# A decoder trunk on one core: the first loads, the order of the first splits, the adder of the first squares, and one pair of unused transposes in each feed-forward block

## The chip, the core and the metric

The kernel runs on one core of a Trainium2 chip. A core has TensorE (PE, matmuls and, in parallel, the loads of their stationary operand, PEld), VectorE (DVE), ScalarE (ACT), GpSimd (POOL), and SyncE (SP), whose queue issues the DMAs here. The metric is device time in microseconds of one execution, median of several runs.

## The reference, cut to what matters

Two layers over 256 tokens of width 1024. Each layer is a half-step SwiGLU block, a mixing block of 16 attention heads of three kinds, and a second half-step SwiGLU block. The change touches the SwiGLU blocks and the first norm.

```python
def _rmsnorm(x, g):
    y = x32 * lax.rsqrt(jnp.mean(x32 * x32, axis=-1, keepdims=True) + RMS_EPS)
    return (y * g.astype(jnp.float32)).astype(x.dtype)

def _swiglu(x, w_gate, w_up, w_down):
    return (jax.nn.silu(x @ w_gate) * (x @ w_up)) @ w_down

for l in range(DEPTH):                                  # DEPTH = 2, D_FF = 2816
    x = x + 0.5 * _swiglu(_rmsnorm(x, ffn1_norm[l]), ffn1_w_gate[l], ffn1_w_up[l], ffn1_w_down[l])
    h = _rmsnorm(x, mix_norm[l])
    ...
    x = x + concatenate([out_a, out_b, out_c]) @ w_out[l]
    x = x + 0.5 * _swiglu(_rmsnorm(x, ffn2_norm[l]), ffn2_w_gate[l], ffn2_w_up[l], ffn2_w_down[l])
return _rmsnorm(x, final_norm)
```

## The kernel before

x is kept transposed in `xs`, 128 partitions by 8 pieces `k` of 256 tokens. All weights are streamed from HBM by SP in chunks of 128x1024 f32 (512 KB), two chunks to a DMA, into five buffers `raw`. Each chunk is split into a high part `whi` (ACT, L160, rounded to fp32r) and the rest `wlo` (DVE, L161); in the mixing block POOL does some of the latter. A piece of x is split in the same way into the operand pair `xx` (ACT L237 multiplies by the norm's scale and rounds, DVE L238 takes the rest). The factor 1/rms is applied after the products.

A product then is a pair of matmuls (`mm2`): `whi` against both halves of `xx` (512 columns), `wlo` against the high half (256 columns). Below, "a pair" is always these two. All TensorE instructions stand in one fixed order, that in which the program writes them.

The four feed-forward blocks are counted 0 to 3 here (two per layer; the mixing blocks stand between 0 and 1 and between 2 and 3, and block 2 follows block 1 directly). In each, `products(i, h)` makes 8 pairs from one chunk, for `i` from 0 to 21 and the halves `h` 0 and 1: 352 pairs `pgu`. The blocks 0 to 2 then make 176 pairs `pdn`, the last one writes 528 matmuls `pfin` of another form. In the middle of `i` = 2 two breaks stand in TensorE's order: after the first pair the sum of squares is taken into a column (`pss`, four matmuls of one column), and nine pairs later two transposes `prow` (L221, `ident` against a 128x2 column broadcast to 128) make the row of 1/rms. In block 0 there is a third one: before `i` = 6 `make_bias` has two matmuls `pu`.

At the start SP issues the norm's scales (`gain`), then x and the first chunk in rows of 1 KB, of 3 KB and of 4 KB by turns (`FIRST`), then the second chunk and the second pair of chunks one by one. Twelve f32 matmuls of `ident` by itself (`warm`) run on TensorE meanwhile. The first pieces are split in the order of the loop at the end of `tile_trunk`. The squares of x for block 0 (`first_squares`) are made by ACT (L246), added up by POOL (`ss`, L251) and folded (`fold`, L255).

What sets the order: `behind` adds an order without a semaphore between two instructions of an engine; apart from that the program's framework places each engine's instructions by its own estimate. PSUM buffers of the tag `at` rotate over four banks, and a new tenant waits for the readers of the one before.

Of the kernel before, what the change touches and what calls it, by code (L numbers as in the profile page):

```python
# [10 lines left out]
F32 = mybir.dt.float32  # L11
F32R = mybir.dt.float32r
AF = mybir.ActivationFunctionType
OP = mybir.AluOpType

P = 128
D = 1024
T = 256
DEPTH = 2
DK = D // P  # L20
# [16 lines left out]
CH = DK * P  # L37
RAW, SPLIT_AHEAD = 5, 3
WARM = 12
AT = (0, 9)  # L40

FIRST = ((0, 1), (1, 4))

LASTK = 3

# [33 lines left out]


@with_exitstack
def tile_trunk(ctx, tc, xT, gains, kvg, sinks, table, onehot, wgu, wdn, winv, wins, wkv, wout, gfin, out):
    nc = tc.nc

    const = ctx.enter_context(tc.tile_pool(name="const", bufs=1))
    wpool = ctx.enter_context(tc.tile_pool(name="wpool", bufs=2))
    act = ctx.enter_context(tc.tile_pool(name="act", bufs=1))
# [10 lines left out]
    def behind(ins, earlier):  # L98

        if earlier is not None:  # L100
            tc.add_manual_dep(ins.ins, earlier.ins.name,
                              mybir.DependencyInfo(mybir.DependencyClass.NoSync, mybir.DependencyReason.DATA),
                              reason="order of issue")
        return ins


    chunks, loads = [], []
# [20 lines left out]
    raws, parts = {}, {}  # L128
# [18 lines left out]
    def split(n, pieces=1, after=None):  # L147

        if n < len(chunks) and n not in parts:
            load(n)  # L150
            w = chunks[n][2]
            parts[n] = halves_of(n)
            step = w // pieces
            for c in range(0, w, step):
                split_part(n, c, c + step, after)

    def split_part(n, a, b, after=None):
        hi, lo = parts[n]
        low = nc.gpsimd if n in shared else nc.vector
        ops = (nc.scalar.copy(hi[:, a:b], raw(n, a, b)),  # L160
               low.tensor_sub(lo[:, a:b], raw(n, a, b), f(hi[:, a:b])))  # L161
        for op, first in list(zip(ops, after or urgent))[:1 if n in shared else 2]:
            behind(op, first)

    def halves_of(n):
        hi = wpool.tile([P, CH], F32R, tag="whi", name=f"whi{n}", bufs=SPLIT_AHEAD + 1)
# [10 lines left out]
        return parts.pop(n)  # L177


    xs = act.tile([P, DK, T], F32, name="xs")  # L180
    x = [xs[:, k, :] for k in range(DK)]
    gain = const.tile([P, (3 * DEPTH + 1) * DK], F32, name="gain")
    nc.sync.dma_start(out=gain, in_=gains)
    room(0)
    for a, b in FIRST:
        nc.sync.dma_start(out=xs[:, a:b, :], in_=xT[:, a:b, :])
        nc.sync.dma_start(out=raws[0][:, 0, 2 * a * P:2 * b * P], in_=loads[0][:, 0, 2 * a * P:2 * b * P])
    nc.sync.dma_start(out=xs[:, DK // 2:, :], in_=xT[:, DK // 2:, :])
    nc.sync.dma_start(out=raws[0][:, 1, :], in_=loads[0][:, 1, :])
    room(1)  # L190
    for j in range(2):
# [6 lines left out]
    ident = const.tile([P, P], F32, name="ident")  # L198
# [2 lines left out]
                            fill=1.0, base=0, channel_multiplier=1)  # L201
    ones = const.tile([P, 1], F32, name="ones")
    nc.vector.memset(ones, 1.0)
    mhalf = const.tile([P, 2], F32, name="mhalf")
    nc.vector.memset(mhalf, -0.5)

    xx = [act.tile([P, 2, T], F32R, name=f"xx{k}") for k in range(DK)]
    xh = [t[:, 0, :] for t in xx]
# [20 lines left out]
    class Norm:  # L229
        def __init__(self, idx):  # L230
            self.idx, self.sums = idx, []

        def g(self, k):
            return gain[:, self.idx * DK + k:self.idx * DK + k + 1]
# [6 lines left out]
        def square(self, k, last=False, after=None):  # L241

            if k % 2 == 0:
                return
            sq = tmp.tile([P, 2, T], F32, tag="sq2", name="sq", bufs=2)
            behind(nc.scalar.activation(sq, xs[:, k - 1:k + 1, :], AF.Square), after)  # L246
            if len(self.sums) == 0 or (last and k == DK - 1):
                self.sums.append(sq)
            else:
                s = tmp.tile([P, 2, T], F32, tag="ss", name="ss", bufs=2)  # L250
                nc.gpsimd.tensor_add(s, self.sums[0], sq)  # L251
                self.sums = [s]
            if k == DK - (3 if last else 1):
                s = tmp.tile([P, T], F32, tag="fold", name="fold", bufs=1)
                nc.gpsimd.tensor_add(s, self.sums[0][:, 0, :], self.sums[0][:, 1, :])  # L255
                self.sums = [s]
            elif k == DK - 1:
                self.sums = [self.sums[0], sq[:, 0, :], sq[:, 1, :]]
# [33 lines left out]
    def mm2(out, whi, wlo, both, first, last):  # L292

        matmul(out, whi, both.rearrange("p a t -> p (a t)"), start=first, stop=False)
        matmul(out[:, :T], wlo, both[:, 0, :], start=False, stop=last)

    def residual(a, b, p, scale, nxt, last=False):
        nc.vector.scalar_tensor_tensor(xs[:, a:b, :], p, scale, xs[:, a:b, :], op0=OP.mult, op1=OP.add)
        if not last:
            for k in range(a, b):  # L300
                nxt.operands(k)
# [5 lines left out]
        nc.vector.tensor_add(a, p[:, :T], b)  # L307
        return a

    def ffn(norm, nxt, last=False, first=None, between=(), at=AT):  # L310
        hs, banks, ws = [], {}, {}

        def products(i, h, start=0, stop=DK):

            if start == 0:
                ws[0] = next_w(ahead=(i, h) not in ((1, 1), (2, 0)))
                if h == 0:
                    for m in range(2):
                        banks[i, m] = bank("pgu", "at" if i % 3 == 2 else "mm")
            whi, wlo = ws[0]  # L320
            for j in range(start, stop):
                k, m = h * DK // 2 + j // 2, j % 2
                c = slice(j * P, (j + 1) * P)
                mm2(banks[i, m], whi[:, c], wlo[:, c], xx[k], k == 0, k == DK - 1)


        products(0, 0)
        products(0, 1)
        if first:
            first()  # L330
        products(1, 0)
        products(1, 1)
        for n in range(2 * DK):
            products(2, n // DK, n % DK, n % DK + 1)
            if n == at[0]:
                col = norm.column()
                for m in range(2):
                    split(cursor[0] + SPLIT_AHEAD - 2 + m)
            if n == at[1]:
                row = rms_row(col)  # L340
        for i in range(FK):
            if i in between:
                between[i]()
            if i > 2:
                products(i, 0)
                products(i, 1)
            g, u = add_halves(banks.pop((i, 0)), "A"), add_halves(banks.pop((i, 1)), "C")
            t = tmp.tile([P, T], F32, tag="A", name="t")
            nc.vector.tensor_mul(t, g, row)  # L349
            s = tmp.tile([P, T], F32, tag="B", name="s")  # L350
            nc.scalar.activation(s, t, AF.Silu)  # L351
            sr = tmp.tile([P, T], F32, tag="B", name="sr")
            nc.gpsimd.tensor_mul(sr, s, row)  # L353
            h = tmp.tile([P, T], F32, tag="h", name="h", bufs=2)
            nc.vector.tensor_mul(h, sr, u)  # L355
            hs.append(act.tile([P, 2, T], F32R, tag=("hh", "hl")[i % 2], name=f"h{i}", bufs=FK // 2))
            nc.scalar.copy(hs[i][:, 0, :], h)  # L357
            nc.vector.tensor_sub(hs[i][:, 1, :], h, f(hs[i][:, 0, :]))
        if last:
            finish(hs)  # L360
            return
        for k in range(DK):
            p = bank("pdn")
            for kk in range(FK):
                j = (k * FK + kk) % DK
                if j == 0:
                    whi, wlo = next_w()
                c = slice(j * P, (j + 1) * P)
                mm2(p, whi[:, c], wlo[:, c], hs[kk], kk == 0, kk == FK - 1)
            nc.vector.scalar_tensor_tensor(x[k], p[:, T:], 0.5, x[k], op0=OP.mult, op1=OP.add)  # L370
            residual(k, k + 1, p[:, None, :T], 0.5, nxt)
            nxt.square(k)
# [405 lines left out]

    norm = Norm(0)
    parts[0], parts[1] = halves_of(0), halves_of(1)  # L780
    for k in range(DK):
        norm.operands(k)
        if k < DK // 2:
            split_part(0, 2 * k * P, 2 * (k + 1) * P)
        elif k % 2:
            split_part(1, (k - 5) * 2 * P, (k - 3) * 2 * P)
    split(2)
    start = norm

    def first_squares():  # L790
# [2 lines left out]

    for l in range(DEPTH):
        nxt = Norm(3 * l + 1)
        ffn(norm, nxt, first=first_squares if l == 0 else None, between={3: load_bias, 6: make_bias} if l == 0 else {})
        norm, nxt = nxt, Norm(3 * l + 2)
        mix(l, norm, nxt)
        norm, nxt = nxt, Norm(3 * l + 3)
        ffn(norm, nxt, last=l == DEPTH - 1)  # L800
        norm = nxt
# [23 lines left out]
def _layout(x, rel_bias_table, ffn1_norm, ffn1_w_gate, ffn1_w_up, ffn1_w_down, mix_norm, w_in, attn_sinks,  # L825
# [7 lines left out]
    g = np.stack([v for l in range(DEPTH) for v in (ffn1_norm[l], mix_norm[l], ffn2_norm[l])] + [final_norm])  # L833
    gu, dn = [], []
    for l in range(DEPTH):
# [11 lines left out]
    winv = np.moveaxis(rv.reshape(DEPTH, P, 4, 2 * VCOLS), 2, 1)  # L847
# [3 lines left out]
    last = wo[:, -LASTK:].reshape(DEPTH, LASTK, P, DK, P).transpose(0, 3, 1, 2, 4).reshape(DEPTH, LASTK, DK, P, P)  # L851
    wo[:, -LASTK:] = last.transpose(0, 1, 3, 2, 4).reshape(DEPTH, LASTK, P, D)
    return {
        "xT": np.moveaxis(x[0].T.reshape(DK, P, T), 0, 1),
        "gains": np.moveaxis(g.reshape(-1, DK, P), 2, 0).reshape(P, -1),
        "kvg": kv_norm_c.T,
        "sinks": attn_sinks[:, HEADS[:NA]].reshape(1, -1),
        "table": rel_bias_table,
# [27 lines left out]
```

## Time and profile before

| | |
|---|---|
| runs, us | 959.44, 965.29, 961.68 (median 961.68) |
| profiled execution, us | 965.39, its span 963.6 |
| TensorE clock granted | 0.998 |
| PE busy in the span | 951.5 us (99%), 5824 matmuls |
| DVE, ACT, POOL busy | 688.2, 553.9, 178.5 us |
| DMA | 174.92 MB, mean 182 GB/s |
| chain that ended last | PE 93%, DVE 2%, ACT 2%, POOL 1%, DMA 1% |

The page counts an engine as busy while it runs an instruction; matmuls overlap, so a busy PE says nothing of how far apart they start. The chain is followed back from the last instruction to what released each step; where it is made of PE alone, PE's own pace sets the time. Timeline rows give start, duration, engine, line, operation, tiles, and in brackets the idle time before with what ended it.

### The profile page before, as it was taken

How to read it: one execution, taken by the hardware profiler on the slowest of the kernel's cores; microseconds unless marked ns; L12 is line 12 of the kernel's file. 1: busy time of each engine (PE TensorE's matmuls, PEld its weight loads, DVE VectorE, ACT ScalarE, POOL GpSimd, SP SyncE). 2: the span in 40 equal slices, each digit the busy share in tenths (PEclk: the TensorE clock that was granted, in tenths of full speed). 3: DMA queues.
4: the chain of work that ended last, by engine and by line, in shares of the span. 5: the costliest groups of instructions: out<-in, count | busy, mean ns of one | idle time of the engine just before them, and what ended most of it. 6: DMA issues, size and time to landing. Idle time of an engine off the chain costs nothing.

```text
span 963.6 us, 15380 instructions
## 1 busy us (share of the span) xinstructions
PE 951.5 (99%) x5824; PEld 839.2 (87%) x5824; DVE 688.2 (71%) x1228; ACT 553.9 (57%) x1024; POOL 178.5 (19%) x154
## 2 busy tenths in 40 slices
PE   8999999999999999999999999999999999999997
PEld 6888888898999888888888888888989988888885
DVE  5787775658847877775668777666696579777544
ACT  6655554446876665654446555544478576556443
POOL 3221110111312221110113112000222042211000
PEclk9999999999999999999999999999999999999999
DMA  9688555563434555545555555555534455555521
GB/s 335 215 296 302 197 195 175 160 213 111 140 128 138 200 192 191 199 175 178 198 186 182 183 208 178 185 188 176 176 109 153 145 187 193 179 198 191 179 85 44
DMA packets 47718, 174.92 MB, mean 182 GB/s; under 512 B 3307, under 2 KB 5883, under 8 KB 47516
## 3 DMA queue, kind: packets, MB, share of 16 engines
q1 hardware_dynamic: 47356, 173.42, 52.1%
q8 instruction: 45, 0.74, 0.3%
q10 hardware_dynamic: 288, 0.52, 0.1%
q14 instruction: 29, 0.24, 0.1%
HBM read 172.86 MB, written 4.22 MB: 184 GB/s over the span
## 4 chain that ended last, share of the span: by engine, by line
PE 93%; DVE 2%; ACT 2%; POOL 1%; DMA 1%; issue 0%; SPq 0%; POOLq 0%; ACTq 0%
PE pgu L218 50%; PE pdn L218 19%; PE pp L218 7%; PE pfin L218 6%; PE pwo L218 5%; PE pv L218 2%; PE po L218 1%; PE pt L221 1%; PE psc L218 1%; DVE acc L563 1%; DMA raw<-wgu 1%; POOL ss L251 1%; DVE m L562 1%; ACT whi L160 1%; ACT e L640 0%
## 5 line engine op out<-in xcount | busy, mean ns | idle before, releaser
L218 PE MATMUL pgu<-xx,whi 128*128 128x512 f32 x1408 | 494.9, 396 | 1.9 <-ACT whi L160 1.9
L161 DVE TENSOR_TENSOR wlo<-raw,whi 128x1024 fp32r<-128x1024 f32 (+3 forms) x314 | 383.2, 1223 | 145.5 <-ACT whi L160 139.0
L160 ACT CAST whi<-raw 128x1024 fp32r<-128x1024 f32 (+2 forms) x322 | 332.7, 1034 | 251.4 <-PE pdn L218 86.2
L218 PE MATMUL pgu<-xx,wlo 128*128 128x256 f32 x1408 | 395.1, 281 | 0.2 <-DVE wlo L161 0.2
L218 PEld LDWEIGHTS pgu<-xx,whi 128*128 128x128 f32 x1408 | 264.1, 188 | 64.5 <-ACT whi L160 2.5
L218 PEld LDWEIGHTS pgu<-xx,wlo 128*128 128x128 f32 x1408 | 266.1, 189 | 0.8 <-DVE wlo L161 0.8
L218 PE MATMUL pdn<-h,whi 128*128 128x512 f32 x528 | 185.5, 396 | 0.0
L353 POOL TENSOR_TENSOR sr<-s,rrow 128x256 f32<-128x256 f32 x88 | 97.9, 1113 | 355.4 <-ACT s L351 355.1
L218 PE MATMUL pdn<-h,wlo 128*128 128x256 f32 x528 | 148.1, 281 | 0.0
L218 PEld LDWEIGHTS pdn<-h,whi 128*128 128x128 f32 x528 | 99.1, 188 | 23.8
L305 ACT COPY b<-pgu 128x256 f32<-128x256 f32 x176 | 65.4, 372 | 80.8 <-PE pgu L218 80.8
L218 PEld LDWEIGHTS pdn<-h,wlo 128*128 128x128 f32 x528 | 99.8, 189 | 0.0
L307 DVE TENSOR_TENSOR a<-pgu,b 128x256 f32<-128x256 f32 x176 | 73.7, 420 | 25.3 <-ACT b L305 24.7
L218 PE MATMUL pp<-xx,whi 128*128 128x256 f32 x480 | 90.8, 289 | 0.0
L218 PEld LDWEIGHTS pp<-xx,whi 128*128 128x128 f32 x480 | 74.2, 191 | 2.7 <-issue 1.7
L218 PE MATMUL pp<-xx,wlo 128*128 128x256 f32 x240 | 67.7, 282 | 0.0
L355 DVE TENSOR_TENSOR h<-sr,a 128x256 f32<-128x256 f32 x88 | 37.4, 425 | 28.9 <-POOL sr L353 28.5
L218 PE MATMUL pfin<-whi,h 128*128 128x512 f32 x176 | 48.8, 391 | 0.0
L218 PE MATMUL pwo<-ohl,whi 128*128 128x256 f32 x256 | 47.7, 287 | 0.0
L357 ACT CAST h<-h 128x256 fp32r<-128x256 f32 x88 | 35.3, 401 | 18.6 <-DVE h L355 18.6
L218 PEld LDWEIGHTS pp<-xx,wlo 128*128 128x128 f32 x240 | 45.8, 191 | 0.0
L351 ACT ACTIVATE s<-t 128x256 f32<-128x256 f32 x88 | 37.4, 425 | 6.0 <-DVE t L349 5.7
(109 smaller groups left out, 796.0 us busy)
## 6 DMA issues: line engine op xcount, KB each, us to landing
raw<-wgu SPq DMA_DIRECT2D x86, 1024.0 KB, 4.9
raw<-wdn SPq DMA_DIRECT2D x44, 1024.0 KB, 4.9
raw<-wins SPq DMA_DIRECT2D x14, 1024.0 KB, 4.9
raw<-wout SPq DMA_DIRECT2D x8, 1024.0 KB, 4.9
raw<-winv SPq DMA_DIRECT2D x4, 776.0 KB, 4.3
w<-u SPq DMA_DIRECT2D x1, 3072.0 KB, 14.5
bias<-w SPq DMA_DIRECT2D x1, 2048.0 KB, 9.3
raw<-wgu SPq DMA_DIRECT2D x3, 512.0 KB, 7.8
```

Source lines behind the costliest of these rows:

```text
L160: ops = (nc.scalar.copy(hi[:, a:b], raw(n, a, b)), low.tensor_sub(lo[:, a:b], raw(n, a, b), f(hi[:, a:b])))
L161: low.tensor_sub(lo[:, a:b], raw(n, a, b), f(hi[:, a:b])))
L218: in_order(nc.tensor.matmul(*a, **kw))
L221: in_order(nc.tensor.transpose(*a))
L251: nc.gpsimd.tensor_add(s, self.sums[0], sq)
L305: nc.scalar.copy(b, p[:, T:])
L307: nc.vector.tensor_add(a, p[:, :T], b)
L351: nc.scalar.activation(s, t, AF.Silu)
L353: nc.gpsimd.tensor_mul(sr, s, row)
L355: nc.vector.tensor_mul(h, sr, u)
L357: nc.scalar.copy(hs[i][:, 0, :], h)
L562: nc.vector.max(out=m8, in_=acc[:, cs])
```

## The change

It does five things.

- `gains` and x become one DRAM tensor with rows of 56 + 2048 f32 to a partition; the tile `xg` holds both. SP's first DMA brings the scales with the first four pieces of x (rows of 4320 bytes), the next the whole first chunk, then the second half of x, the second chunk, and the second pair of chunks as before.
- `mhalf` is set first, and an ACTIVATE on it that nobody reads (`idle`) is issued ahead of all loads.
- The first splits go half by half: four `xx`, then four quarters of chunk 0, then four `xx`, then four quarters of chunk 1, each ordered behind the last; chunk 2 behind those.
- The adds of the squares of the first norm are done by DVE instead of POOL.
- `step()` writes two transposes of `mhalf`, broadcast to 128 columns, against `ident` into an `at` bank that nobody reads. It is called once in each feed-forward block: in block 0 after `i` = 6, `h` = 0, in the others after three pairs of `i` = 3, `h` = 0.

```diff
-FIRST = ((0, 1), (1, 4))
+STEPS, STEPS0 = ((3, 0, 3),), ((6, 1, 0),)
+GAINS = (3 * DEPTH + 1) * DK
...
-    xs = act.tile([P, DK, T], F32, name="xs")
+    xg = act.tile([P, GAINS + DK * T], F32, name="xs")
+    gain, xs = xg[:, :GAINS], xg[:, GAINS:].rearrange("p (k t) -> p k t", t=T)
     x = [xs[:, k, :] for k in range(DK)]
-    gain = const.tile([P, (3 * DEPTH + 1) * DK], F32, name="gain")
-    nc.sync.dma_start(out=gain, in_=gains)
+    mhalf = const.tile([P, 2], F32, name="mhalf")
+    nc.vector.memset(mhalf, -0.5)
+    nc.scalar.activation(const.tile([P, 2], F32, name="idle"), mhalf, AF.Copy, scale=mhalf[:, 0:1])
+    cut = GAINS + DK // 2 * T
     room(0)
-    for a, b in FIRST:
-        nc.sync.dma_start(out=xs[:, a:b, :], in_=xT[:, a:b, :])
-        nc.sync.dma_start(out=raws[0][:, 0, 2 * a * P:2 * b * P], in_=loads[0][:, 0, 2 * a * P:2 * b * P])
-    nc.sync.dma_start(out=xs[:, DK // 2:, :], in_=xT[:, DK // 2:, :])
+    nc.sync.dma_start(out=xg[:, :cut], in_=xT[:, :cut])
+    nc.sync.dma_start(out=raws[0][:, 0, :], in_=loads[0][:, 0, :])
+    nc.sync.dma_start(out=xg[:, cut:], in_=xT[:, cut:])
     nc.sync.dma_start(out=raws[0][:, 1, :], in_=loads[0][:, 1, :])
...
+            self.adder = nc.gpsimd if idx else nc.vector
...
-                nc.gpsimd.tensor_add(s, self.sums[0], sq)
+                self.adder.tensor_add(s, self.sums[0], sq)
...
-                nc.gpsimd.tensor_add(s, self.sums[0][:, 0, :], self.sums[0][:, 1, :])
+                self.adder.tensor_add(s, self.sums[0][:, 0, :], self.sums[0][:, 1, :])
...
+    def step():
+        p = bank("step", "at")
+        for b in range(2):
+            transpose(p[:, b * P:(b + 1) * P], mhalf[:, b:b + 1].to_broadcast([P, P]), ident)
...
             for j in range(start, stop):
+                if (i, h, j) in steps:
+                    step()
...
-    for k in range(DK):
-        norm.operands(k)
-        if k < DK // 2:
-            split_part(0, 2 * k * P, 2 * (k + 1) * P)
-        elif k % 2:
-            split_part(1, (k - 5) * 2 * P, (k - 3) * 2 * P)
-    split(2)
+    ops = (None, None)
+    for n in range(2):
+        for k in range(n * DK // 2, (n + 1) * DK // 2):
+            norm.operands(k)
+            for op, earlier in zip(norm.ops, ops):
+                behind(op, earlier)
+            ops = norm.ops
+        for c in range(0, CH, CH // 4):
+            ops = split_part(n, c, c + CH // 4, ops)
+    split(2, after=ops)
```

ACT at the start of the program, before: `xx` is the operand pair of a piece of x, `whi` a part of a chunk, `raw` its buffer.

```order
L237 ACT_TABLE_LOAD
L237 ACTIVATE xx_103<-xs,gain 128x256
L160 CAST whi_126<-raw_75 128x256
L237 ACTIVATE xx_104<-xs,gain 128x256
L237 ACTIVATE xx_105<-xs,gain 128x256
L160 CAST whi_126<-raw_75 128x256 x2
L237 ACTIVATE xx_106<-xs,gain 128x256
L160 CAST whi_126<-raw_75 128x256
```

And after the change.

```order
L190 ACT_TABLE_LOAD
L190 ACTIVATE idle<-mhalf 128x2
L243 ACTIVATE xx_101<-xs 128x256
L243 ACTIVATE xx_102<-xs 128x256
L243 ACTIVATE xx_103<-xs 128x256
L243 ACTIVATE xx_104<-xs 128x256
L163 CAST whi_124<-raw_77 128x256 x4
```

The table load moves in front of an instruction that reads only `mhalf`, and the four pieces of x come ahead of the four quarters of the first chunk instead of between them.

DVE from the second chunk on to the sum of squares, after the change (`wlo_161` and `wlo_165` are chunks 2 and 3, `wlo_187` is chunk 4, `ss` and `fold` the adds of the squares).

```order
L164 TENSOR_TENSOR wlo_127<-raw_77,whi_126 128x256 x4
L164 TENSOR_TENSOR wlo_161<-raw_82,whi_160 128x1024
L257 TENSOR_TENSOR ss<-sq 128x512
L164 TENSOR_TENSOR wlo_165<-raw_82,whi_164 128x1024
L257 TENSOR_TENSOR ss<-ss,sq 128x512 x2
L261 TENSOR_TENSOR fold<-ss 128x256
L164 TENSOR_TENSOR wlo_187<-raw_85,whi_186 128x1024
```

The four adds stood on POOL, ahead of `rcol`; now they stand between the splits of chunks 2, 3 and 4 on DVE.

PE in block 0, after the change: the end of `i` = 6, `h` = 0 and the beginning of `h` = 1.

```order
L223 MATMUL pgu<-xx_104,whi_474 128x512
L223 MATMUL pgu<-xx_104,wlo_475 128x256
L226 MATMUL step<-ident,mhalf 128x128 x2
L223 MATMUL pgu<-xx_105,whi_515 128x512
L223 MATMUL pgu<-xx_105,wlo_516 128x256
```

Two matmuls stand between two pairs that followed each other before. In the blocks 1 to 3 the same two stand between the third and the fourth pair of `i` = 3; nothing else in PE's order differs.

## Rows read from the trace of the kernel before

**Rows 1.** The page, part 1: busy us (share of the span) xinstructions.

```profile
PE 951.5 (99%) x5824; PEld 839.2 (87%) x5824; DVE 688.2 (71%) x1228; ACT 553.9 (57%) x1024; POOL 178.5 (19%) x154
```

**Rows 2.** The chain in order of time: start us, us, what.

```profile
2.59 5.81 DMA raw<-wgu
...
14.57 1.80 POOL ss L251
...
20.98 1.60 POOL fold L255
22.62 0.61 PE pss L218 x4
...
137.50 62.19 PE pdn L218 x352
...
315.80 109.54 PE pgu L218 x620
...
503.03 107.48 PE pgu L218 x620
```

**Rows 3.** Waits of PE from 0 to 60 us: us in total, times, longest.

```profile
PE pgu L218 <- ACT whi L160: 1.9, 2, 1.3
...
PE pss L218 <- POOL fold L255: 1.0, 1, 1.0
```

**Rows 4.** The timeline from 0 to 40 us.

```profile
0.74 0.39 SPq L183 DMA_DIRECT2D gain<-gains  x1
...
1.35 5.49 PE L218 MATMUL warm<-ident 128*128 128x128 f32 x24 [1.35 <-POOL ident L200]
...
3.76 1.28 ACT L237 ACT_TABLE_LOAD   x1 [3.76 <-DMA xs<-xT]
...
6.50 0.59 PE L218 MATMUL pgu<-xx,whi 128*128 128x512 f32 x1
...
8.42 0.71 ACT L160 CAST whi<-raw 128x256 fp32r<-128x256 f32 x2
...
9.75 1.71 ACT L237 ACTIVATE xx<-xs,gain 128x256 fp32r<-128x256 f32 x4
...
10.32 1.67 DVE L238 SCALAR_TENSOR_TENSOR xx<-xs,gain,xx 128x256 fp32r<-128x256 f32 x4
...
11.99 1.30 DVE L161 TENSOR_TENSOR wlo<-raw,whi 128x512 fp32r<-128x512 f32 x2
...
12.92 1.03 ACT L160 CAST whi<-raw 128x1024 fp32r<-128x1024 f32 x1
...
13.85 0.63 ACT L246 ACTIVATE sq<-xs 128x512 f32<-128x512 f32 x1
...
15.46 1.99 DVE L161 TENSOR_TENSOR wlo<-raw,whi 128x1024 fp32r<-128x1024 f32 x1 [0.25 <-ACT whi L160]
...
18.52 1.23 DVE L161 TENSOR_TENSOR wlo<-raw,whi 128x1024 fp32r<-128x1024 f32 x1 [1.07 <-ACT whi L160]
```

**Rows 5.** Windows: us, busy (x) of PE, PEld, DVE, ACT, POOL; PEclk, DMA share, GB/s.

```profile
3.25:5.25 2.00, 2.00 (x11) 2.00 (x11) 0.00 (x0) 1.47 (x2) 0.00 (x0) 1.00 0.90 130
...
6.50:13.00 6.50, 4.39 (x21) 2.96 (x21) 4.97 (x12) 5.49 (x14) 0.00 (x0) 1.00 1.02 412
```

**Rows 6.** DMA issues from 689.5 to 694 us: xcount, KB, us to landing.

```profile
raw<-wins SPq DMA_DIRECT2D x1, 512.0 KB, 3.4
```

**Rows 7.** PE groups, 26.05 to 26.2 us: xcount, busy us, mean ns, idle.

```profile
L218 PE MATMUL pgu<-xx,whi 128*128 128x512 f32 x1 | 0.4, 403 | 0.0
```

**Rows 8.** The same, 315.13 to 315.3 us.

```profile
L218 PE MATMUL pgu<-xx,whi 128*128 128x512 f32 x1 | 0.4, 398 | 0.0
```

**Rows 9.** PE's timeline, 26.1 to 27.3 us: block 0's transposes `prow`.

```profile
26.23 0.28 PE L218 MATMUL pgu<-xx,wlo 128*128 128x256 f32 x1
26.35 0.38 PE L221 MATMUL prow<-ident,rcol 128*128 128x128 f32 x2
...
26.93 0.39 PE L218 MATMUL pgu<-xx,whi 128*128 128x512 f32 x1
```

More of the change, by code (lines that the diff above doesn't have):

```diff
@@ L81, in tile_trunk @@
 @with_exitstack
-def tile_trunk(ctx, tc, xT, gains, kvg, sinks, table, onehot, wgu, wdn, winv, wins, wkv, wout, gfin, out):
+def tile_trunk(ctx, tc, xT, kvg, sinks, table, onehot, wgu, wdn, winv, wins, wkv, wout, gfin, out):
     nc = tc.nc
@@ L163, in split_part @@
             behind(op, first)
+        return ops
     def halves_of(n):
@@ L203, in tile_trunk @@
     nc.vector.memset(ones, 1.0)
-    mhalf = const.tile([P, 2], F32, name="mhalf")
-    nc.vector.memset(mhalf, -0.5)
     xx = [act.tile([P, 2, T], F32R, name=f"xx{k}") for k in range(DK)]
@@ L308, in add_halves, with ffn @@
         return a
-    def ffn(norm, nxt, last=False, first=None, between=(), at=AT):
+    def ffn(norm, nxt, last=False, first=None, between=(), at=AT, steps=STEPS):
         hs, banks, ws = [], {}, {}
@@ L795, in tile_trunk @@
         nxt = Norm(3 * l + 1)
-        ffn(norm, nxt, first=first_squares if l == 0 else None, between={3: load_bias, 6: make_bias} if l == 0 else {})
+        if l == 0:
+            ffn(norm, nxt, first=first_squares, between={3: load_bias, 6: make_bias}, steps=STEPS0)
+        else:
+            ffn(norm, nxt)
         norm, nxt = nxt, Norm(3 * l + 2)
@@ L853, in _layout @@
     return {
-        "xT": np.moveaxis(x[0].T.reshape(DK, P, T), 0, 1),
-        "gains": np.moveaxis(g.reshape(-1, DK, P), 2, 0).reshape(P, -1),
+        "xT": np.concatenate([np.moveaxis(g.reshape(-1, DK, P), 2, 0).reshape(P, -1),
+                              np.moveaxis(x[0].T.reshape(DK, P, T), 0, 1).reshape(P, -1)], axis=1),
         "kvg": kv_norm_c.T,
```

## The prediction

> **What bounds the kernel now.** I read the page's busy times first: PE is busy for 951.5 of 963.6 us [rows 1], so only two things can move the end: idle time of PE at either end, and the pace of PE itself. The chain says where the first lies: up to 22.62 us it runs through a DMA, ACT, and then POOL's adds of the squares, and behind `pss` it is PE nearly throughout [rows 2]. The waits of PE name it from the other side: two waits for `whi`, 1.9 us, and one of 1.0 us for `fold` [rows 3]. The timeline gives the first product at 6.50 us [rows 4]. From there to `pss` stand 33 pairs (chunks 0 to 3 and one). At the pace below they need 33 x 0.353 = 11.65 us, and they take 22.62 - 6.50 = 16.12: 4.5 us are lost there.
>
> For the pace, the chain's long PE pieces are divided by their pairs (two matmuls each). Block 0's `pdn`: 62.19 us / 176 = 353.4 ns. Block 1 behind `prow`: 109.54 / 310 = 353.4. Block 2 behind `prow`: 107.48 / 310 = 346.7 [rows 2]. The instructions are alike and nobody is waited for, yet there are two paces, 6.7 ns a pair apart, and each holds for hundreds of pairs, across chunks and from `pgu` into `pdn`. In the slow one the wide matmul's length goes round in three pairs, 403, 398, 395 ns; in the fast one it is 391 throughout. A pace changes only where the stream is broken. Before `prow` of block 0 the last wide matmul was one of 403 ns [rows 7], and behind it the pace was fast; the same row stands before block 2's `prow`, fast behind it too. Before block 1's it was one of 398 ns [rows 8], and the slow pace went on. In block 3 the pace was fast before `prow` and stayed so. So I read the result of a two-transpose break from the place in the round of three at which it falls: after 403 it ends the slow pace (2 of 2), after 398 it does not (1 of 1), and in the fast pace it does no harm (1 of 1).
>
> **The change, part by part.**
>
> *First loads.* SP's first DMA is issued at 0.74 us as before [rows 4]. It is now 553 KB in rows of 4320 bytes. The nearest row is a DMA of 512 KB issued to an idle queue: 3.4 us to landing [rows 6]; the 5% more add 0.1. So x's first half is there at 0.74 + 3.5 = 4.2 us. What follows is queued behind it, 524 KB each at 412 GB/s [rows 5], 1.27 us: chunk 0 at 5.5, the second half of x at 6.8, chunk 1 at 8.0, chunk 2 at 9.3. Before, the same queue moved only 130 GB/s from 3.25 to 5.25 us, with the rows of 1 and 3 KB [rows 5]. Bounds: at 412 GB/s from the first microsecond on, everything 0.9 us earlier; with the same 2 us at 130 instead of 412 GB/s again, 2 x (412 - 130) / 412 = 1.4 us later.
>
> *Table load.* 1.28 us, begun at 3.76, when x had landed [rows 4]. It now waits for a memset only, and lies before 4.2 us under the load: nothing of it is left on the path. If it did stay there, the first split would start at 5.5.
>
> *Order of the splits.* ACT takes 1.71 us for four `xx` and about 0.35 for a quarter (0.71 for two); DVE 1.67 and, from 1.30 for two halves, about 0.35 as well, the first some 0.4 [rows 4]. ACT: `xx` 4.25 to 5.96, chunk 0's quarters to 7.4, `xx` to 9.1, chunk 1's quarters from 9.1, the first done at 9.5, all at 10.45; one `sq` 0.63, chunk 2 1.03 [rows 4], done at 12.1. DVE follows by half a microsecond: the first `wlo` quarter at 6.9, chunk 1's first at 10.0, and chunk 2 at 12.1 + 1.23 = 13.4. PE is held by `warm` until about 6.45 in any case (its rows end at 6.84, the last overlapping [rows 4]), starts there, and has its first narrow matmul at 6.9, as before. Then 8 pairs to 9.7; 0.3 us of waiting for chunk 1's `wlo`; 8 pairs; 0.5 us for chunk 2's; 16 pairs and one: `pss` at 19.2 instead of 22.62. **Minus 3.4 us.** With the loads' bounds put through the same steps `pss` comes at 18.2 or at 20.6: minus 4.4 to minus 2.0.
>
> *Adds on DVE.* POOL took 1.80 us for one add of 128x512 and 1.60 for the fold [rows 2]; PE waited for the last [rows 3]. On DVE a two-input operation of that size costs 0.65 (half of 1.30 [rows 4]), so three and a fold are about 2.4 us. Between chunk 2 at 13.4 and `pss` DVE has `ss` to 14.05, chunk 3 to 15.3, two `ss` to 16.6, `fold` to 17.0: 2.2 us before `pss` asks. Behind them in DVE's queue stands chunk 4, done at 18.2, which PE asks for at 19.0: the cover is 0.8 us, and what goes beyond it would be PE's. One thing comes back: a split of 1.23 us took 1.99 while POOL's add ran [rows 4]. I take zero beyond the wait that is already in the 3.4.
>
> *The steps.* Each is two transposes of the form of `prow`. In block 0 the start of the narrow matmul before `prow` and that of the second wide one behind it are 26.93 - 26.23 = 0.70 us apart [rows 9]; without it, one pair and a narrow-to-wide distance of 0.12 would be 0.47. So 0.23 each, **plus 0.9 us** for four. The bank that each writes has been read long before in the blocks 1 to 3; in block 0 its reader is DVE's sum for the first half of `i` = 5, eight pairs of `i` = 6 back, and in the trace it was over by then.
>
> What they give hangs on where they fall. In block 1 the step comes nine pairs behind `prow`; the wide matmul there is one of 403 ns. In block 0 it comes eight pairs behind `pu`, and there too it is 403 (the row of [rows 7] stands the same at 49.36 and 318.47 us). Both then are breaks of the kind that ended the slow pace. Block 0: 248 pairs `pgu` and 176 `pdn` are left, 424 x 6.7 ns = **minus 2.8 us**. Block 1: 301 + 176, and 33 of block 2 up to its own `pss`, 510 x 6.7 = **minus 3.4 us**. Blocks 2 and 3 are fast already, so there the step is only its price. Bounds: no gain at all, or a loss where a step falls in the fast pace (below).
>
> **The sum** against the profiled execution's own time: 965.39 - 3.4 + 0.9 - 2.8 - 3.4 = **956.7 us**. That execution is the longest of those shown; against their median, 961.68, it is 0.5% less. The three runs spread by 5.85 us, about what the slow stretches of the blocks 0 and 1 are worth together; if some ran with one of them fast, the median holds part of this gain already.
>
> **The rivals.**
>
> *The steps are only a price.* A rule stands beside it: the Trainium skill, "TensorE: Matmul & The Clock Gate", section "Back-to-back issue gap", gives the isolated gap of a matmul from its columns alone, which would make a pair 325 ns (an estimate from its table) whatever stood before; no run here shows that pace. What speaks against the rival is that one stream has two paces and that breaks changed them [rows 2, 7, 8]; what speaks for it is that two breaks are few. Then 965.39 - 3.4 + 0.9 = 962.9.
>
> *One of the two blocks stays slow.* The new start shifts where `pss` of block 0 falls in the round, and the round behind `pu` may differ; block 1 comes out of a mixing block with hundreds of short waits. 956.7 + 2.8 = 959.5, or + 3.4 = 960.1.
>
> *The loads stumble as before.* The long rows meet the same slow stretch that rows of 3 KB met: 1.4 us later, 958.1.
>
> *The other side: a step breaks the fast pace.* In block 2 a step that turned it slow would cost 477 pairs x 6.7 = 3.2 us, in block 3 301 x 6.7 = 2.0. With no gain in the blocks 0 and 1: 962.9 + 5.2 = 968.1, slower than before. It decides from 2.5 us on, that is with block 2 alone. For it: `pu`, a longer break, did turn the fast pace of block 0 into the slow one. Against it: `prow` of block 3, the same two transposes, did not.
>
> **How the numbers follow.** The sum 0.58; one block stays slow 0.18; the loads stumble 0.08; only a price 0.06; the other side 0.04; more than the sum (the better loads, and no waits for chunks 1 and 2: below 955) 0.06. The range 953.5 to 961.0 leaves out the price and the other side, and takes in the bounds of the loads on both sides of the sum. About 1%, 9.6 us, is what a measurement of this kernel can tell from no change. Faster by more needs under 952.1 against the median, or under 955.7 if before is measured like its profiled execution: 0.10. Slower by more needs 971.3: 0.02. The rest, 0.88, is within.
>
> **What would show it.** In the profile after: `ACT_TABLE_LOAD` over before 3 us; first `xx` near 4.2; `pss` near 19.2 with no wait for `fold`; block 0's `pdn` in 61.0 us instead of 62.19, and block 1's pgu piece in some 107.7; wide matmuls of 391 ns behind each step. The prediction is wrong if the first `xx` starts after 5.6, if a wait for chunk 4's `wlo` takes the place of that for `fold`, or if `pdn` of block 0 or 1 still takes 62.2.

## The result, and the profile after

| | before | after |
|---|---|---|
| median of 5 runs each, us | 961.7 (959.44 to 965.29) | 968.37 (968.29 to 968.54) |
| ratio to before, 95% interval | | 1.0057 [1.0031, 1.0082] |
| profiled execution, us | 965.39, its span 963.6 | 968.34, its span 966.5 |

So the change costs 0.6%. By the 1% named above that is no change, but it lies 7.4 us over the upper end of the range, 961.0, and on the other side of before. Each ratio, here and below, is to runs of before taken beside the kernel in question; the median of before was 961.7 to 964.1 us in them.

The page of after, part 1, to be laid beside [rows 1]: PE is busy 5.8 us longer, with eight matmuls more.

```profile
PE 957.3 (99%) x5832; PEld 839.7 (87%) x5832; DVE 687.8 (71%) x1234; ACT 553.5 (57%) x1027; POOL 170.7 (18%) x150
```

The start went as it was meant to. Four rows of the timeline of after from 0 to 40 us (start us, us, what):

```profile
0.73 1.28 ACT L190 ACT_TABLE_LOAD   x1 [0.73 <-PEq L895]
...
4.52 1.71 ACT L243 ACTIVATE xx<-xs 128x256 fp32r<-128x256 f32 x4 [2.20 <-DMA xs<-xT]
...
12.91 0.69 DVE L257 TENSOR_TENSOR ss<-sq 128x512 f32<-128x512 f32 x1
...
16.17 0.42 DVE L261 TENSOR_TENSOR fold<-ss 128x256 f32<-128x256 f32 x1
```

The first DMA of after, then the window from 3.25 to 5.25 us (columns as in [rows 5]): 419 GB/s where before had 130.

```profile
xs<-xT SPq DMA_DIRECT2D x1, 540.0 KB, 3.8
```

```profile
3.25:5.25 2.00, 2.00 (x11) 2.00 (x11) 0.19 (x1) 0.73 (x2) 0.00 (x0) 1.00 1.04 419
```

Of PE's waits in the first 60 us, where before had those of [rows 3], one is left, that of the warm-up for `ident`:

```profile
PE warm L223 <- POOL ident L207: 1.4, 1, 1.4
```

The loss is behind the start. The chain of after:

```profile
18.99 0.34 PE pss L223 x4
...
22.78 19.06 PE pgu L223 x108
...
134.05 62.19 PE pdn L223 x352
...
315.12 106.35 PE pgu L223 x602
421.47 62.19 PE pdn L223 x352
...
502.54 106.35 PE pgu L223 x602
608.89 62.19 PE pdn L223 x352
...
789.98 106.35 PE pgu L223 x602
...
934.48 20.78 PE pfin L223 x89
```

And three pieces of before that [rows 2] did not need:

```profile
610.52 61.01 PE pdn L218 x352
...
787.49 107.47 PE pgu L218 x620
...
932.23 20.21 PE pfin L218 x89
```

Every `pdn` of after takes 62.19 us, 353.4 ns a pair, and each of the three long `pgu` pieces 106.35 us for 301 pairs, 353.3 ns. No step ended the slow pace, and the blocks 2 and 3, fast before, are slow now. The step of block 0 even fell into a fast stretch, the eight pairs behind `pu`, and the slow pace began behind it: the wide matmuls from 44 to 45.9 us, ahead of the step, and from 47 to 50.2 us.

```profile
L223 PE MATMUL pgu<-xx,whi 128*128 128x512 f32 x7 | 2.5, 392 | 0.0
```

```profile
L223 PE MATMUL pgu<-xx,whi 128*128 128x512 f32 x11 | 3.9, 397 | 0.0
```

The slow pace is also not the old one: before's wide matmuls went round in three (403, 398, 395 ns), after's go by turns (0.40 and 0.39 us), the spacing of the pairs being 345 and 361 ns. Even `pfin`, which the change doesn't touch, became longer.

The two spans, stretch by stretch (after minus before, us): up to `pss` -3.6; `pss` to `prow` of block 0 -0.3; `prow` to `pu` +0.3; the rest of block 0 +0.2; first mixing block -0.7; block 1 +0.3; block 2 +3.4; second mixing block -0.6; block 3 up to `pfin` +2.4; `pfin` +1.5; the tail +0.1. That is +2.9 net, the 966.5 - 963.6 of the spans.

What had changed that nobody had written? The tiles had moved. In the built programs the tile of the scales left the constants' pool and went in front of x, and `mhalf` and `idle` changed places with it. So the weight tiles `whi` and `wlo` start 192 bytes lower than before and the operand tiles `xx` and `h` 32 bytes higher. All these tiles have sizes that are multiples of 256 bytes, so in one kernel every weight tile has the same remainder modulo 256, and every operand tile too: before 64 and 64, after 128 and 96. Below, "distance" is operand minus weight modulo 256: 0 before, 224 after. These places are read from the programs, not from a trace. Padding changes no engine's order of instructions: in the built programs every padded kernel below has that of its unpadded version.

### The profile page after: what moved, and what is told of

Its sections match the earlier page's. It is cut to its first block, busy times and chain, and to the rows that moved or that the text cites. A ratio compares the mean times of both kernels' runs of the same rounds, so it can differ in the third digit from the quotient of the medians.

```text
span 966.5 us, 15393 instructions
## 1 busy us (share of the span) xinstructions
PE 957.3 (99%) x5832; PEld 839.7 (87%) x5832; DVE 687.8 (71%) x1234; ACT 553.5 (57%) x1027; POOL 170.7 (18%) x150
## 4 chain that ended last, share of the span: by engine, by line
PE 96%; DVE 2%; ACT 1%; issue 0%; POOL 0%; POOLq 0%; ACTq 0%
PE pgu L223 52%; PE pdn L223 19%; PE pp L223 7%; PE pfin L223 6%; PE pwo L223 5%; PE pv L223 2%; PE po L223 1%; PE pt L226 1%; PE psc L223 1%; DVE acc L576 1%; PE warm L223 1%; DVE m L575 1%; ACT e L653 0%; PE pi L223 0%; PE pss L223 0%
## 5 line engine op out<-in xcount | busy, mean ns | idle before, releaser
L164 DVE TENSOR_TENSOR wlo<-raw,whi 128x1024 fp32r<-128x1024 f32 (+2 forms) x316 | 380.7, 1208 | 147.9 <-ACT whi L163 140.8
```

## The experiments

Each kernel computes the whole output. Where an edit says "no steps" it is `STEPS, STEPS0 = (), ()`. Padding is written as a longer tile of which the old part is used.

**First: the places, or the steps and the new order?** *After with the places of before.*

```diff
-    xg = act.tile([P, GAINS + DK * T], F32, name="xs")
+    xg = act.tile([P, GAINS + DK * T + 8], F32, name="xs")[:, :GAINS + DK * T]
-    mhalf = const.tile([P, 2], F32, name="mhalf")
+    mhalf = const.tile([P, 2 + 48], F32, name="mhalf")[:, 0:2]
```

> The changed kernel with padding alone: 192 bytes more in the small constants and 32 behind x, so that the weight tiles and the operand tiles xx and h start again at 64 modulo 128 bytes, as before the change (the change had moved the weights to 0 and xx and h to 96 modulo 128). Theory A (where the operands lie sets which slow round TensorE can fall into, and whether two transposes end it): the slow round is again of three pairs (361, 349, 350 ns) and the steps end it in the blocks 0 and 1, 955.5 to 958.5 us, pdn of block 0 in 61.0 us. Theory B (the new start and the steps themselves put the stream into the round of two, addresses don't matter): 968 to 969 us, the round of two (345, 361) as in the changed kernel.

964.69 us, 1.0025 [1.0014, 1.0036]: neither theory's number. The round of three is back, and block 2 is fast, but block 0, block 1 and, unlike before, block 3 are slow. Its chain:

```profile
22.85 19.07 PE pgu L223 x108
...
134.16 62.19 PE pdn L223 x352
...
607.40 61.01 PE pdn L223 x352
...
787.73 106.35 PE pgu L223 x602
```

So the places decide which round there is. But this run also tests the prediction's rule on breaks, at the old places. The wide matmul just before `prow` of block 0, in the window from 22.2 to 22.33 us, and `prow` itself from the timeline:

```profile
L223 PE MATMUL pgu<-xx,whi 128*128 128x512 f32 x1 | 0.4, 403 | 0.0
```

```profile
22.47 0.38 PE L226 MATMUL prow<-ident,rcol 128*128 128x128 f32 x2
```

It is one of 403 ns, as in [rows 7], and the 54 pairs behind `prow` take 19.07 us, 353.1 ns each: slow. `prow` of block 1 also came behind 403 ns (window from 311.7 to 311.78 us), and the slow pace went on there too.

```profile
L223 PE MATMUL pgu<-xx,whi 128*128 128x512 f32 x1 | 0.4, 403 | 0.0
```

*Before with only the operand tiles moved, by 32 bytes, as in after.*

```diff
-    xs = act.tile([P, DK, T], F32, name="xs")
+    xs = act.tile([P, DK * T + 8], F32, name="xs")[:, :DK * T].rearrange("p (k t) -> p k t", t=T)
```

> The kernel before with 32 unused bytes behind x, so that xx and h start at 96 modulo 128 as after the change; the weights stay at 64, nothing else moves. Theory A: a round of two pairs, the blocks 2 and 3 slow behind their prow (796 pairs x 6.7 ns = 5.3 us on the profile of before), pfin some 1.4 us longer: 967 to 972 us. Theory B: as before, 959 to 966 us, round of three pairs.

958.64 us, 0.9961 [0.9947, 0.9974]: outside what either theory said, faster instead of slower. Its chain:

```profile
22.56 0.61 PE pss L218 x4
...
135.67 61.01 PE pdn L218 x352
...
603.19 61.01 PE pdn L218 x352
...
779.28 107.47 PE pgu L218 x620
...
924.88 20.78 PE pfin L218 x89
```

All four blocks run at 346.7 ns a pair, with no step and with before's late `pss`. Thirty-two bytes behind x do what the steps were thought to do. Groups of PE from 150 to 190 us show the two paces: first this kernel, then after.

```profile
L218 PE MATMUL pdn<-h,whi 128*128 128x512 f32 x117 | 40.6, 390 | 0.0
```

```profile
L223 PE MATMUL pdn<-h,whi 128*128 128x512 f32 x114 | 40.3, 397 | 0.0
```

*After without steps, and the old places without steps* (the same padding as in the first edit).

```diff
-STEPS, STEPS0 = ((3, 0, 3),), ((6, 1, 0),)
+STEPS, STEPS0 = (), ()
```

> The changed kernel without the four steps, addresses as in the changed kernel. If a step breaks the fast pace that stands behind pu (eight pairs at 346.7 ns in the changed kernel's trace): 424 pairs at 346.7 and four steps of 0.23 us less, 968.4 - 2.8 - 0.9 = 964.6 us. If the steps are a price only: 967.4. If they were what ends a slow pace anywhere: over 968.4.

> As e1 without the steps: the new start with the old addresses. Theory A: the pace is that of the kernel before (blocks 0 and 1 in part slow, 2 and 3 fast), less 3.6 us for the start: 957 to 962 us, and 0 to 5 us above e1, which is what the steps are worth. Theory B: about 967.

967.45 us, 1.0053 [1.0036, 1.007], the number of "a price only", and 963.87, 1.0028 [1.0012, 1.0044], between the two theories. Taking the four steps out gives back 968.37 - 967.45 = 0.9 us and 964.69 - 963.87 = 0.8, and no long stretch changes its pace with them: the first keeps `pdn` at 62.18 to 62.19 us throughout, the second is slow in the blocks 0, 1 and 3 and fast in 2, as with steps. A piece of the first, then two of the second (blocks 2 and 3):

```profile
608.23 62.19 PE pdn L223 x352
```

```profile
499.58 107.47 PE pgu L223 x620
...
784.04 109.53 PE pgu L223 x620
```

In the second, `prow` of block 3 too came behind a wide matmul of 403 ns (window from 783.4 to 783.5 us) and left the slow pace as it was.

**Second: which place counts, that of the weights, that of the operands, or their distance?** Edits on after: `+ 48` and `+ 16` of padding (weights at 64, operands at 96) without and with steps; `+ 48` and none behind x (64 and 32, distance 224 as in after) without steps. And before with 16 elements behind the scales and 24 behind x:

```diff
-    xs = act.tile([P, DK, T], F32, name="xs")
+    xs = act.tile([P, DK * T + 24], F32, name="xs")[:, :DK * T].rearrange("p (k t) -> p k t", t=T)
-    gain = const.tile([P, (3 * DEPTH + 1) * DK], F32, name="gain")
+    gain = const.tile([P, (3 * DEPTH + 1) * DK + 16], F32, name="gain")[:, :(3 * DEPTH + 1) * DK]
```

> The changed kernel without the steps, padded so that the weight tiles start at 64 modulo 128 bytes and xx and h at 96, the two that e2 had (the changed kernel has 0 and 96, the kernel before 64 and 64). If the two starts set the pace: 346.7 ns a pair in all blocks, and e2's time less what the new start gives (pss at 19.0 instead of 22.6 us): 958.6 - 3.6 = 955.0 us. If e2's pace came from something else in the kernel before: 961 to 968.

> As e5 with the four steps. If a step is a price only: e5 + 0.9 us. If it breaks the pace even here: up to 5 to 10 us more than e5. If it gives something: under e5.

> As e5 with xx and h at 32 modulo 128, the weights at 64: the distance from weight to operand is 96 as in the changed kernel, both starts differ from it. If the distance alone matters: the round of two pairs, about 967.5 us. If it matters that the operand lies 32 bytes off a multiple of 64 while the weights lie on an odd multiple of 64: as e5, about 955.

> The kernel before, nothing changed but padding (96 bytes behind the norm's scales, 64 behind x), so that its weight and operand tiles start where the changed kernel has them, at 0 and 96 modulo 128. If the starts alone cost the changed kernel its time: the round of two pairs (345, 361 ns) nearly everywhere, pfin some 1.5 us longer, and the changed kernel's time plus its gain at the start less the steps: 968.4 + 3.6 - 0.9 = 971.1 us. If the loss came from the new start or the steps: 959 to 966 as before.

955.07 us (0.9901 [0.9872, 0.993]) without steps, 955.73 (0.9908 [0.9879, 0.9936]) with them: with weights at 64 and operands at 96 all blocks are fast, and the steps are a price of 0.7 us. The chain of the one without steps:

```profile
22.73 18.73 PE pgu L223 x108
...
131.80 61.01 PE pdn L223 x352
...
599.12 61.01 PE pdn L223 x352
...
775.23 107.48 PE pgu L223 x620
...
920.82 20.77 PE pfin L223 x89
```

Operands at 32 instead of 96, distance 224 at other places than after's: 967.56 us, 1.0034 [1.0017, 1.005], after's round of 345 and 361 ns, and after's chain:

```profile
134.16 62.18 PE pdn L223 x352
...
933.84 20.77 PE pfin L223 x89
```

The last of the four was meant to give before the places of after, and missed its number: 966.82 us, 1.0024 [1.0008, 1.004], and neither of the two paces but a third, 61.60 us / 176 = 350.0 ns. The places had been counted modulo 128; modulo 256 this kernel's weights lie at 128 and its operands at 224, a distance of 96, and not 224 as in after. (The expectation's text names the two paddings the wrong way round; the edit has 64 bytes behind the scales and 96 behind x.) Modulo 128 the two kernels are alike, and their paces are not: that miss shows that 128 is too small a period.

```profile
136.66 61.60 PE pdn L218 x352
...
608.33 61.60 PE pdn L218 x352
```

**Third: the distance again at other weights, and three distances not seen yet.** Without steps: after's own weights with 64 bytes behind x (128 and 160, distance 32), and `+ 48` with `+ 24`, `+ 40`, `+ 56` behind x (weights at 64, distances 64, 128, 192).

```diff
-    xg = act.tile([P, GAINS + DK * T], F32, name="xs")
+    xg = act.tile([P, GAINS + DK * T + 16], F32, name="xs")[:, :GAINS + DK * T]
```

> As e5 with weights and operand tiles both moved by 64 bytes against it: weights at 128 modulo 256, xx and h at 160, so both starts are new and the distance from weight tile to operand tile is 32 modulo 256 as in e2, e5 and e6. If the distance alone sets the pace: 346.7 ns a pair in all blocks, 955 us as e5. If the starts themselves count: another pace, 960 to 968.

> As e5 with the distance from weight tile to operand tile 64 modulo 256 instead of 32 (weights at 64, xx and h at 128). If every distance has a pace of its own: a steady pace between 346.7 and 353.4 ns in all blocks, 955 to 968 us. If only the place inside 64 bytes counts: as distance 0, both paces, round of three, 959 to 964.

> As e10 with distance 128 modulo 256. If the distance counts modulo 128: both paces as at distance 0, 959 to 964 us. If modulo 256 or more: a pace of its own, 955 to 968.

> As e10 with distance 192 modulo 256. If distances just below a multiple of 256 are bad as 224 is: 353.3 ns, about 967 us. If 224 is bad for its odd 32 bytes: a pace like that of 64 or of 0, 955 to 964.

954.97 us (0.9918 [0.99, 0.9936]), 966.65 (1.0033 [1.0015, 1.005]), 964.38 (1.0009 [0.9999, 1.002]) and 965.94 (1.003 [1.0016, 1.0044]). The chain of each, in that order:

```profile
131.88 61.01 PE pdn L223 x352
```

```profile
133.99 62.18 PE pdn L223 x352
```

```profile
133.21 61.80 PE pdn L223 x352
...
930.33 20.78 PE pfin L223 x89
```

```profile
134.04 62.19 PE pdn L223 x352
...
931.89 20.40 PE pfin L223 x89
```

The first of them is the sharpest pair of the study: against after without steps (967.45) it differs by 64 unused bytes behind x, and by 12.5 us. So do the two kernels of the second group with weights at 64 and no steps, taken side by side: 955.07 with operands at 96, 967.56 with operands at 32. That is the pace: 1408 pairs `pgu` and 528 `pdn` at 6.7 ns are 13.0 us, and 0.5 us come back because the faster PE waits for `fold` in the blocks 1 and 3:

```profile
PE pss L223 <- POOL fold L261: 0.5, 2, 0.2
```

| distance modulo 256 | kernels (weights, operands) | ns a pair (`pdn` / 176) |
|---|---|---|
| 0 | before; after's code at before's places, with and without steps (64, 64) | 353.4 or 346.7, by blocks |
| 32 | three at (64, 96), one at (128, 160) | 346.7 |
| 64 | (64, 128) | 353.3 |
| 96 | (128, 224) | 350.0 |
| 128 | (64, 192) | 351.1 |
| 192 | (64, 0) | 353.4 |
| 224 | after, with and without steps (128, 96); (64, 32) | 353.3 to 353.4 |

The table is of the long stretches. At distance 224 short pieces run at 346.7 ns too, such as the nine pairs from `pss` to `prow` of block 0 and, in after, the eight behind `pu`; at 32 no stretch behind the first `pss` is slow in any of the four traces.

## Why the prediction was wrong

**The start: right.** `pss` was forecast for 19.2 us and came at 18.99; the first `xx` for 4.2 and came at 4.52 (the 540 KB, the 553 of the prediction in units of 1024, took 3.8 us to land, not 3.5); `fold` done at 17.0, done at 16.17 + 0.42 = 16.6; the table load is under the first load; no wait of PE for `whi`, `fold` or chunk 4 is left, and the loads did not stumble (419 GB/s). Some of the nearness is luck. The terms as written add up to 19.3; PE's first narrow matmul came at 7.13 instead of 6.9, the waits of 0.3 and 0.5 us for the chunks 1 and 2 shrank to about 0.1 and 0.2 (349 to 357 ns between wide matmuls grow to 449 and 518 there), and the pairs behind them ran at 346.7 ns and not at 353. The bound of the loads "0.9 us earlier" can't be worked out from the rows named beside it, but nothing measured hangs on it. The gain was 3.6 us where 3.4 stood in the sum, and it is real in the end as well: at one pace, that of distance 32, the new start makes the difference between a span of 956.8 us (before, moved) and 952.9 (after's code without steps), 3.9 us.

**The steps' price: right.** 0.9 us was forecast; 0.9, 0.8 and 0.7 were measured at three placements.

**What the steps give, -2.8 and -3.4: wrong, both terms.** The step that failed is "after 403 it ends the slow pace (2 of 2)". It was a rule from two cases, and it doesn't hold at the very places for which it was read: with them, three breaks behind a 403 ns matmul (two in after at before's places, one in the same without steps) left the slow pace as it was. In after itself the round of three that the rule reads is not there at all. "In the fast pace it does no harm (1 of 1)" fails as well: in after the step of block 0 and `prow` of block 0 stand between fast pairs and slow ones. Of the prediction's signs of being wrong one came true, `pdn` of the blocks 0 and 1 at 62.19 us. What ended the slow pace in four kernels was no break but a distance of 32 bytes. The prediction saw rightly that two paces of like instructions are worth 6.7 ns a pair, and then looked for the cause in the order of the instructions, which it could see, and not in the operands' places, which it had not looked at.

**What was missing: the places.** The prediction costed the scales' move as a DMA only, and so put the move of all tiles behind it at nothing. Of the forecast 965.39 - 8.7 = 956.7 against 968.34, 11.6 us, the two terms that failed are 6.2. The rest are stretches that were to stay as they were: block 2 +3.2 without its step, block 3 up to `pfin` +2.2, `pfin` +1.5, less 1.3 in the mixing blocks, and some tenths of the start and of the blocks 0 and 1. None of these is the work of an instruction that the change added; with 64 bytes behind x the same code without steps is at 954.97.

**The rivals.** "The steps are only a price" (962.9) named what the steps do, but not the time, since it too kept the old pace in the blocks 2 and 3. "The other side" (968.1) is near the number by accident: it held a step in block 2 and one in block 3 guilty, and without any step these blocks are as slow. The Trainium skill, "TensorE: Matmul & The Clock Gate", section "Back-to-back issue gap", works out a matmul's isolated gap from its columns alone; an estimate from its table, 325 ns a pair, has no term for the places. The runs differ: 346.7 to 353.4 ns by distance, for the same columns, and the measurement decides.

**What the better kernel is.** The new start without steps at distance 32 is the fastest version run: 954.97 and 955.07 us at two placements, ratios 0.9918 [0.99, 0.9936] and 0.9901 [0.9872, 0.993].

**What stays open.** Why the distance sets the pace: that the reads of the moving and of the stationary operand get in each other's way is an idea that no run tested. The padding behind x also moves the working tiles of DVE, ACT and POOL, but none of the three sets the pace by its work: taken two pairs at a time in long stretches of after (137 to 185, 340 to 400, 425 to 470 and 520 to 600 us), the mean is 353.3 ns a pair both where DVE is idle and where it is busy throughout, and the same holds for ACT and for POOL; in the kernel of 954.97 us it is 346.7 ns either way. The DMAs run all the time, so no trace tells their part. At distance 0, what chooses between the two paces: before's runs spread over 5.9 us and those of after's code at before's places without steps over 4.2 (963.49 to 967.72), kernels at other distances over 0.25 to 2.8, so the choice may differ from run to run, but no run was made to settle it. Distance 160 and steps finer than 32 bytes were not tried. Whether 256 bytes is the period is in part seen: counted in full, the distance is 256 bytes longer in after's code with weights at 64 and operands at 96 than in before moved, at the same 346.7 ns, and 256 longer in after's code at before's places than in before, with the same round of three; the two placements at 224 have the same full distance and say nothing of it.

## What to carry to other kernels

A change that adds, drops or resizes any SBUF tile also moves all tiles that are allocated behind it, and here the places alone are worth 12.5 us of 967, more than all that the change meant to do gave (3.6 us). Where PE is the bound and a stretch of like matmuls has two paces, note the start of the stationary and of the moving tile in both programs before looking for a cause in the order; compare a change at one distance, by padding, and then try a few paddings for their own sake. And a rule drawn from two cases in one trace is a guess: one kernel that holds all but the rule's condition still would have shown it.

## What the runs showed of the hardware

The pace of a stream of matmuls that alternates its stationary tile (512 and 256 columns by turns) depends on where its two operands start in SBUF. In the long stretches it is 346.7 ns a pair at a distance of 32 bytes modulo 256, 350.0 at 96, 351.1 at 128, 353.3 to 353.4 at 64, 192 and 224, either 346.7 or 353.4 at 0, with a granted clock of 0.998 to 0.999 in all of them. PE waits for no engine in them. The Trainium skill, "SBUF — State Buffer", section "Who interferes with whom", has the reads of the moving operand and of the weights on two independent ports of PE; the runs don't contradict two ports, but the two tiles' places are not independent in their effect on time. For `pfin`, where `h` is stationary and the weights move, the best distance is another one: its last 89 matmuls took 20.21 us at distance 0, 20.40 at 192, and 20.77 to 20.87 elsewhere, 0.6 us that a kernel at distance 32 gives away there. Why is open as well.
